# Final transposes in front of the last unit, and caches and memory laid out as the kernel uses them

## The chip, the cores and the metric

The kernel runs on one core of one Trainium2 chip. The metric is the device time of one execution in microseconds (us), lower is better. On a core several engines work side by side, each through its own queue in order: TensorE (PE; its weight loads are listed as PEld) multiplies, VectorE (DVE) and ScalarE (ACT) do elementwise work, GpSimd (POOL) does a little of it, SyncE (SP) only issues transfers. A transfer (DMA) is issued by SP, ACT or POOL and then runs on the core's 16 DMA engines. An engine that reaches an instruction whose inputs are not there waits, and everything behind it in its queue waits too.

## What is computed

Two layers of a diffusion trunk, for 128 context tokens and 128 latent tokens with the same weights. Cut to what matters here:

```
for l in range(2):
    x = x + 0.5*gate1 * swiglu(mod1(rms_norm(x)))          # FFN 1
    u = mod2(rms_norm(x)); z = u @ w_in                    # q, k, v, Fourier and mLSTM parts, gates
    context: keys and values are k, v;                      new_cache_k/v[l] = k, v
    latent:  keys = [cache_k | rope(k)], values = [cache_v | v], mLSTM starts from state_C, state_n, state_m
    p  = softmax(q1 k1) - lambda * softmax(q2 k2);  a_out = rms_norm(p @ v)
    x = x + gate2 * (sum of three gated branches) @ w_out
    x = x + 0.5*gate3 * swiglu(mod3(rms_norm(x)))          # FFN 2
y = rms_norm(x, g_final)                                   # (tokens, 1024), for both groups
```

All matrices are float32. The kernel multiplies each with the weight and the activation split into a high part (`hi`, reduced precision) and the rest (`lo`), in three products (`mm3`).

## The kernel before

**Layout and units.** Activations are kept transposed, channels on the 128 partitions, both groups' 256 tokens side by side. Weights come in chunks of mostly 1 MB (`raw`, 6 buffers) that SP loads. A chunk is cut into units; a unit is split (`split_one`) by an ACT copy (`whi`, L1523) and a DVE subtraction (`wlo`, L1524) into one of 6 pairs of buffers, and PE then runs its products: 24 of 256 columns (L166 to L168, called from `prod8`), or 12 of 512 (L760 to L762, in `aform`). A pair of buffers comes free when PE has used it, and so the ACT and DVE queues hold splits that wait for PE.

**Order.** A list of steps is recorded once, in order; each step issues its products, then refills splits. Between them, in the mixer, generators called lanes (`attn_lane`, `gate_lane`, `mlstm_lane`, `four_lane`) do the rest of the layer: at a fixed place (`mid`, half way through each unit, and after each unit) one lane is moved on to its next `yield`. What a lane issues there stands at that place in every queue. An earlier `yield` or one less therefore moves all that follows in this lane, on every engine. On DVE, steps of the adaptive modulation (L319) stand between the others.

**The mixer's start.** `first` does the four q units. `loads2` then issues on ACT's queue the loads of `cache_k` and `cache_v` (tile `ckv`) and of `state_C` (`C0`). The units k0 to k3 follow, then v0, the gates (24 products, `zgh`), v1 to v3, the Fourier units. `attn_lane` does, in this order: four PE transposes of `ckv` (half way through k2), a DVE copy of them into `kl`; `swap`, four copies from `q` into `kl` by ACT's queue, which exchange halves for the rotary step; `rope` of q on DVE, which needs them; `swap` of k, which needs the DVE to be done with `kl`; four PE transposes of k and a copy, which POOL's queue writes to `new_cache_k`; the context scores; `softmax`, whose result is `pc` (L873); four transposes of `pc`. `gate_lane` ends with eight transposes of `C0` into `c0t`. POOL's queue also loads the gate weights (`zgw`, L698).

**Transfers wait for transfers.** The transfers of SP and ACT take turns at eight semaphores. An issue waits for the transfer that used its semaphore before, in the issuing engine's queue.

**The end.** The last steps are the six units of `w_ffn2_out` for channel blocks 6 and 7. After a block's last unit, `residual` adds it to x (DVE, L570), `square` (ACT) squares it, POOL adds the square to `nsum`; block 7's stays apart (`nsq`). `block` scales y by `g_final` (DVE, L422). `fin` sums the squares on PE (L163), takes the root (`root`: DVE, then POOL), transposes the eight blocks of y for each group, 16 transposes, and scales each four of them by `rstd` on ACT or DVE into a tile that SP writes out.

Of the kernel before, what the change touches and what calls it, by code (L numbers as in the profile page):

```python
# [17 lines left out]
P = 128  # L18
D = 1024
KD = D // P  # L20
T = 128
# [101 lines left out]
def trunk_kernel(ctx: ExitStack, tc: tile.TileContext, a: dict):  # L123
# [568 lines left out]
    def add_mixer(l, norm, norm_next, mods_):  # L692
# [3 lines left out]
        def loads():  # L696
            M["zgw"] = tmp([P, KD, 16], "zgw", bufs=1)
            po.dma_start(out=M["zgw"], in_=w_in[:, 4096:4112].rearrange("(k p) f -> p k f", p=P))  # L698

        def loads2():  # L700
            ac.preload_act_table_set("natural_log_exp_and_others")
            M["ck"] = blk([P, 2, H, P], "ckv")
            nc.scalar.dma_start(out=M["ck"][:, 0], in_=a["cache_k"][0, l].rearrange("h s d -> s h d"))
            nc.scalar.dma_start(out=M["ck"][:, 1], in_=a["cache_v"][0, l].rearrange("h s d -> s h d"))
            M["C0"] = blk([P, 2, H, P], "C0")
            nc.scalar.dma_start(out=M["C0"], in_=a["state_C"][0, l].rearrange("d h v k -> v d h k"))
            gh, gl = M["gh"], M["gl"] = blk([P, KD, 104], "zgh", F32R), blk([P, KD, 104], "zgl", F32R)
            po.memset(gh.bitcast(F32), 0.0)
            po.memset(gl.bitcast(F32), 0.0)
            for gi, c0 in enumerate((0, 64, 32, 96)):  # L710
                s = M["zgw"][:, :, 4 * gi:4 * gi + 4].unsqueeze(2).to_broadcast([P, KD, 2, 4])
                hi, lo = (x[:, :, c0:c0 + 8].rearrange("p k (i h) -> p k i h", i=2) for x in (gh, gl))
                ve.tensor_copy(hi, s)
                ve.tensor_sub(lo, s, hi.bitcast(F32))
# [88 lines left out]
        def attn_lane():  # L803
            q = M["q"]
            ql = q[:, :, T:]
            kl = blk([P, H, 256], "kl")
            yield
            yield
            t = pa([P, H, P])
            for h in range(H):  # L810
                trans(t[:, h, :], M["ck"][:, 0, h, :])
            yield
            ve.tensor_copy(kl[:, :, 0:128], t)
            cosb = cst[:, C_COS:C_COS + 128].unsqueeze(1).to_broadcast([P, H, T])
# [21 lines left out]
            yield  # L836
            t = pa([P, H, P])
            for h in range(H):
                trans(t[:, h, :], k[:, h, 0:T])
            yield  # L840
            kn = t2([P, H, P], "kctx")
            ac.copy(kn, t)
            po.dma_start(out=a["new_cache_k"][0, l].rearrange("h s d -> s h d"), in_=kn)
            yield
# [115 lines left out]
            for h in range(H):  # L960
                for c in range(2):
                    vv = M["ck"][:, 1, h, :] if c == 0 else M["v"][:, 1, h * P:(h + 1) * P]
                    mm(o[:, h, :], pTl[h // 2][:, 2 * (h % 2) + c, :], vv, start=(c == 0), stop=(c == 1))
# [42 lines left out]
        def gate_lane():  # L1006
# [69 lines left out]
            for g in range(2):  # L1076
                M["w"][g] = blk([P, 2, H, T], f"w{g}")
                for d in range(2):
# [5 lines left out]
                    for h in range(H):  # L1084
                        ac.activation(M["w"][g][:, d, h, :], E[:, h, :], AF.Exp,
                                      bias=gT[:, g, 32 * d + h:32 * d + h + 1])
            yield
            c0t = M["c0t"] = blk([P, H, 2, 129], "c0t")
            ve.tensor_copy(c0t[:, :, :, 128],
                           parT[1][:, 96 + 8 * l:104 + 8 * l].rearrange("p (d h) -> p h d", d=2))  # L1090
            for d in range(2):
                t = pb([P, H, P])
                for h in range(H):
                    trans(t[:, h, :], M["C0"][:, d, h, :])
                yield
                ve.tensor_copy(c0t[:, :, d, 0:128], t)

# [345 lines left out]
    for l in range(DEPTH):  # L1443
# [3 lines left out]
        add_ffn(l, 2, norms[l, 2], norms[l + 1, 0], ADA.get((l, "ffn2")))  # L1447

    def fin():
        nf = norms[DEPTH, 0]  # L1450
        nf.stats()
        while held:
            held.pop(0)()
        outs = ("y_prompt", "y_sample")
        for i in range(2):
            for g in range(2):
                t = (pa, pm)[g]([P, 4, P])
                for r in range(4):
                    trans(t[:, r, :], nf.y[i][:, r, G[g]])
                o = t2([P, 4, P], "yo")  # L1460
                if g == 0:
                    ac.activation(o, t, AF.Copy, scale=nf.rstd[:, g:g + 1])
                else:
                    ve.tensor_scalar(o, t, nf.rstd[:, g:g + 1], None, op0=ALU.mult)  # L1464
                nc.sync.dma_start(out=a[outs[g]][0, :, i * 512:(i + 1) * 512], in_=flat(o))

    add(fin)

# [67 lines left out]
    for s in steps:  # L1536
# [16 lines left out]
        for fn in late:  # L1553
# [4 lines left out]

_INS = ["x_prompt", "x_sample", "cache_k", "cache_v", "state_C", "attn_lambda", "w_ada", "w_ffn1_in",
        "w_ffn1_out", "w_ffn2_in", "w_ffn2_out", "w_in", "w_branch_gate", "w_br_attn", "w_br_four",  # L1560
        "w_br_mlstm", "w_out"]
_OUTS = [("y_prompt", (1, T, D)), ("y_sample", (1, T, D)),
         ("new_cache_k", (1, DEPTH, H, T, 128)), ("new_cache_v", (1, DEPTH, H, T, 128)),
         ("new_state_C", (1, DEPTH, 2, H, 128, 128)), ("new_state_n", (1, DEPTH, 2, H, 128)),
# [3 lines left out]
def _arrays(inputs):  # L1568
# [6 lines left out]
    wt = inputs["w_ada"].reshape(DEPTH, D, N_MOD, KD // 2, 2, P)  # L1575
    arrays["w_adaT"] = np.ascontiguousarray(wt.transpose(0, 2, 3, 5, 4, 1))
    return arrays

# [16 lines left out]
```

## Time and profile before

| | |
|---|---|
| median of 3 runs | 1338.78 us (1338.4 to 1339.75) |
| profiled execution | 1340.14 us |
| its span (first to last instruction) | 1338.4 us |
| PE busy | 1306.4 us, 98% |
| DVE busy | 1038.2 us, 78% |
| ACT busy | 659.8 us, 49% |
| POOL busy | 68.0 us, 5% |
| moved by DMA | 304.70 MB, 228 GB/s mean |

Busy is the sum of an engine's instructions over the span. PE's products overlap, so the time one of them takes of the stream is the distance between two starts, not its own duration. A wait is listed with the instruction that ended it. PEclk is the granted clock of TensorE as a share of 2.4 GHz: 0.5 is 1.2 GHz.

### The profile page before, as it was taken

Reading aid. Unit: us, or ns where it says so; the run is one execution under the profiler, and the core shown is the slowest. Engines: PE = TensorE matmul, PEld = TensorE weight load, DVE = VectorE, ACT = ScalarE, POOL = GpSimd, SP = SyncE. Lnnn points to the kernel's source line nnn. Section 1 sums busy time; section 2 is a strip of 40 time slices with the busy share of each in tenths; the row PEclk is TensorE's granted clock in tenths of the full one; section 3 lists DMA queues with packets and bytes.
Section 4 is the critical chain, followed back from the end, with each engine's and each line's share of the span. In section 5 each row is a group of like instructions: output and inputs, shape, how many; then the busy total and the mean of one; then the engine's idle time right before and its main releaser. Section 6 shows DMA issues by size and latency. Waiting matters only on the chain. (4 is left out here: it accounts for less than half of the span.)

```text
span 1338.4 us, 25512 instructions
## 1 busy us (share of the span) xinstructions
PE 1306.4 (98%) x10584; PEld 1256.4 (94%) x10584; DVE 1038.2 (78%) x1652; ACT 659.8 (49%) x1026; POOL 68.0 (5%) x88
## 2 busy tenths in 40 slices
PE   8999999899999998999999999989999999999998
PEld 6999999788999997999999999988999899999998
DVE  5798897687678888888979988876677889895553
ACT  4654444565554454444445544455555446554442
POOL 0000001000000020000000000110000001000001
PEclk9999999899999999999999999999999999999999
DMA  9999774745567538887748977856446766495520
GB/s 377 373 336 357 242 260 163 239 139 189 190 227 260 191 130 302 277 297 264 249 155 280 302 256 252 279 167 191 158 135 200 273 228 208 164 310 188 168 96 32
DMA packets 221587, 304.70 MB, mean 228 GB/s; under 512 B 5584, under 2 KB 194272, under 8 KB 214176
## 3 DMA queue, kind: packets, MB, share of 16 engines
q1 hardware_dynamic: 213760, 295.93, 65.8%
q10 hardware_dynamic: 6640, 4.20, 1.2%
q0 software_dynamic: 1072, 2.95, 0.6%
q8 instruction: 83, 1.36, 0.4%
q14 instruction: 32, 0.26, 0.1%
HBM read 298.85 MB, written 3.15 MB: 226 GB/s over the span
## 5 line engine op out<-in xcount | busy, mean ns | idle before, releaser
L1524 DVE TENSOR_TENSOR wlo<-raw,whi 128x1024 fp32r<-128x1024 f32 (+1 forms) x428 | 507.3, 1192 | 219.3 <-ACT whi L1523 217.1
L1523 ACT CAST whi<-raw 128x1024 fp32r<-128x1024 f32 (+1 forms) x428 | 434.6, 1024 | 298.7 <-PE pm L167 211.9
L166 PE MATMUL pm<-uh,whi 128*128 128x256 f32 x1904 | 546.9, 287 | 0.0
L167 PE MATMUL pm<-ul,whi 128*128 128x256 f32 x1904 | 538.3, 283 | 1.0 <-DVE ul L495 0.9
L168 PE MATMUL pm<-uh,wlo 128*128 128x256 f32 x1904 | 538.2, 283 | 0.4 <-DVE wlo L1524 0.3
L166 PEld LDWEIGHTS pm<-uh,whi 128*128 128x128 f32 x1904 | 363.0, 191 | 12.6 <-issue 7.1
L167 PEld LDWEIGHTS pm<-ul,whi 128*128 128x128 f32 x1904 | 362.7, 190 | 2.5 <-DVE ul L495 2.1
L168 PEld LDWEIGHTS pm<-uh,wlo 128*128 128x128 f32 x1904 | 362.4, 190 | 0.9 <-DVE wlo L1524 0.8
L319 DVE CUSTOM_DVE_ANT_0 junkw<-raw,cb 128x1024 bf16<-128x1024 f32 x192 | 233.7, 1217 | 0.0
L168 PE MATMUL pm<-hh,wlo 128*128 128x256 f32 x640 | 179.6, 281 | 0.0
L166 PE MATMUL pm<-hh,whi 128*128 128x256 f32 x640 | 179.5, 280 | 0.0
L167 PE MATMUL pm<-hl,whi 128*128 128x256 f32 x640 | 179.5, 280 | 0.0
L168 PEld LDWEIGHTS pm<-hh,wlo 128*128 128x128 f32 x640 | 120.7, 189 | 0.0
L166 PEld LDWEIGHTS pm<-hh,whi 128*128 128x128 f32 x640 | 120.6, 188 | 0.0
L167 PEld LDWEIGHTS pm<-hl,whi 128*128 128x128 f32 x640 | 120.5, 188 | 0.0
L413 POOL TENSOR_TENSOR nsum<-nsum,nsq 128x256 f32<-128x256 f32 x36 | 36.1, 1002 | 816.7 <-issue 436.7
L657 ACT ACTIVATE silu<-pm 128x512 f32<-128x512 f32 x38 | 22.7, 596 | 54.9 <-PE pm L168 54.9
L411 ACT ACTIVATE nsq<-xT 128x256 f32<-128x256 f32 x42 | 17.5, 417 | 53.2 <-DVE xT L570 53.1
L177 ACT CAST hh<-silu 128x512 fp32r<-128x512 f32 x37 | 22.8, 620 | 41.4 <-DVE silu L659 41.4
L570 DVE SCALAR_TENSOR_TENSOR xT<-pm,mod,xT 128x128 f32<-128x128 f32 x96 | 28.7, 342 | 17.4 <-PE pm L168 17.3
L760 PE MATMUL pm<-whi,uh 128*128 128x512 f32 x96 | 39.3, 410 | 0.0
L761 PE MATMUL pm<-wlo,uh 128*128 128x512 f32 x96 | 37.9, 395 | 0.0
(339 smaller groups left out, 1751.4 us busy)
## 6 DMA issues: line engine op xcount, KB each, us to landing
raw<-w_ffn_in SPq DMA_DIRECT2D x82, 1024.0 KB, 6.8
raw<-w_adaT SPq DMA_DIRECT2D x48, 1024.0 KB, 5.0
raw<-w_ffn_out SPq DMA_DIRECT2D x32, 1024.0 KB, 5.0
raw<-w_in SPq DMA_DIRECT2D x32, 1024.0 KB, 5.8
raw<-w_ada SPq DMA_DIRECT2D x24, 1024.0 KB, 6.9
raw<-w_branch_gate SPq DMA_DIRECT2D x24, 1024.0 KB, 5.2
raw<-w_ffn_out SPq DMA_DIRECT2D x16, 768.0 KB, 6.0
raw<-w_out SPq DMA_DIRECT2D x8, 1024.0 KB, 5.0
```

Source lines behind the costliest of these rows:

```text
L166: pe.matmul(out, sh, mh, start=start, stop=False)
L167: pe.matmul(out, sh, ml, start=False, stop=False)
L168: pe.matmul(out, sl, mh, start=False, stop=stop)
L177: ac.copy(hi, src)
L319: ve.tensor_tensor_reduce(junkw, u.raw()[:, 0, :], cb[:, g, :], 1.0, 0.0, op0=ALU.mult, op1=ALU.add, accum_out=o[:, k, g:g + 1])
L413: eng.tensor_add(self.sum, self.sum, sq)
L570: ve.scalar_tensor_tensor(xT[:, k, G[g]], ps[:, G[g]], gate[:, k, g:g + 1], xT[:, k, G[g]], op0=ALU.mult, op1=ALU.add)
L657: ac.activation(st["s"], st["a"], AF.Silu)
L760: pe.matmul(ps[g], xh[:, G[g]], wh, start=(k == 0), stop=False)
L761: pe.matmul(ps[g], xh[:, G[g]], wl, start=False, stop=False)
L1523: ac.copy(u.hi, r)
L1524: ve.tensor_sub(u.lo, r, u.hi.bitcast(F32))
```

## The change

`cache_k`, `cache_v`, `state_C` and the gate columns of `w_in` are handed to the kernel by the host in the order in which the kernel uses them (`cache_kT`, `cache_vT`, `state_CT`, `w_inz`), and `new_cache_k` is written with channels first and turned on the host. So the transposes of `ckv`, of k and of `C0`, with their copies, are gone: `cache_kT` is loaded straight into `kl`, `state_CT` into `c0t`, and k is written out from its own tile. The gate weights and `new_cache_k` go by ACT's queue and no longer by POOL's. In `fin`, the transposes of y's first four blocks stand as a step of their own (`early`) in front of the last unit; those of blocks 4 and 5 stand between the two sums, those of blocks 6 and 7 behind them.

```
         def loads():
-            po.dma_start(out=M["zgw"], in_=w_in[:, 4096:4112].rearrange("(k p) f -> p k f", p=P))
+            nc.scalar.dma_start(out=M["zgw"], in_=a["w_inz"][l])
         def loads2():
-            M["ck"] = blk([P, 2, H, P], "ckv")
-            nc.scalar.dma_start(out=M["ck"][:, 0], in_=a["cache_k"][0, l].rearrange("h s d -> s h d"))
-            nc.scalar.dma_start(out=M["ck"][:, 1], in_=a["cache_v"][0, l].rearrange("h s d -> s h d"))
-            M["C0"] = blk([P, 2, H, P], "C0")
-            nc.scalar.dma_start(out=M["C0"], in_=a["state_C"][0, l].rearrange("d h v k -> v d h k"))
+            M["cv"] = blk([P, H, P], "cv")
+            nc.scalar.dma_start(out=M["cv"], in_=a["cache_vT"][l])
+            M["c0t"] = blk([P, H, 2, 129], "c0t")
+            nc.scalar.dma_start(out=M["c0t"][:, :, :, 0:128], in_=a["state_CT"][l])
...
             kl = blk([P, H, 256], "kl")
-            yield
-            yield
-            t = pa([P, H, P])
-            for h in range(H):
-                trans(t[:, h, :], M["ck"][:, 0, h, :])
-            yield
-            ve.tensor_copy(kl[:, :, 0:128], t)
+            nc.scalar.dma_start(out=kl[:, :, 0:128], in_=a["cache_kT"][l])
+            yield
+            yield
...
             swap(k[:, :, T:])
             yield
-            t = pa([P, H, P])
-            for h in range(H):
-                trans(t[:, h, :], k[:, h, 0:T])
-            yield
-            kn = t2([P, H, P], "kctx")
-            ac.copy(kn, t)
-            po.dma_start(out=a["new_cache_k"][0, l].rearrange("h s d -> s h d"), in_=kn)
+            nc.scalar.dma_start(out=a["new_cache_k"][0, l], in_=k[:, :, 0:T])
             yield
...
-            c0t = M["c0t"] = blk([P, H, 2, 129], "c0t")
+            c0t = M["c0t"]
...
-            for d in range(2):
-                t = pb([P, H, P])
-                for h in range(H):
-                    trans(t[:, h, :], M["C0"][:, d, h, :])
-                yield
-                ve.tensor_copy(c0t[:, :, d, 0:128], t)
...
+    def turn(i, g, rs):
+        if (i, g) not in yT:
+            yT[i, g] = (pa if i == 0 else (pd, pb)[g])([P, 4, P])
+        for r in rs:
+            trans(yT[i, g][:, r, :], norms[DEPTH, 0].y[i][:, r, G[g]])
+    def early():
+        for g in range(2):
+            turn(0, g, range(4))
     def fin():
         nf = norms[DEPTH, 0]
-        nf.stats()
+        ss = pb([P, 2])
+        for g in range(2):
+            mm(ss[:, g:g + 1], nf.sum[:, G[g]], ones[:, 0:1], start=g == 0, stop=False)
+        for g in range(2):
+            turn(1, g, (0, 1))
         while held:
             held.pop(0)()
+        for g in range(2):
+            mm(ss[:, g:g + 1], nf.last[:, G[g]], ones[:, 0:1], start=False, stop=g == 1)
+        for g in range(2):
+            turn(1, g, (2, 3))
+        nf.root(ss)
...
-                t = (pa, pm)[g]([P, 4, P])
-                for r in range(4):
-                    trans(t[:, r, :], nf.y[i][:, r, G[g]])
+                t = yT[i, g]
...
+    steps.insert(len(steps) - 1, Step(early, pump=False))
     add(fin)
```

On DVE in the first layer's mixer, where the context softmax ends (`pc`) beside the gate lane (`gpk`, whose running sums and maxima are the rows from a 40x256 operation to the 8x128 ones), before:

```order
L1037 SCALAR_TENSOR_TENSOR gpk_3080<-gpk_3080,gb 40x256
L1041 SCALAR_TENSOR_TENSOR gpk_3080<-gpk_3080 8x128
L1041 SCALAR_TENSOR_TENSOR gpk_3080<-gpk_3080,gb 8x128
L1041 SCALAR_TENSOR_TENSOR gpk_3080<-gpk_3080 8x128
L1041 SCALAR_TENSOR_TENSOR gpk_3080<-gpk_3080,gb 8x128
L1524 TENSOR_TENSOR wlo<-raw_2956,whi 128x1024
L319 ISA junkw,mod_7_103<-raw_2841,cb 128x1024
L319 ISA mod_7_103 128x1
L868 RECIPROCAL rs<-sm 128x8
L870 TENSOR_TENSOR cf<-sm,rs 128x4
L871 TENSOR_SCALAR cf<-cf,lamn 128x4
L873 SCALAR_TENSOR_TENSOR pc<-e_3177,cf,pc 128x128 x4
```

and after:

```order
L1528 TENSOR_TENSOR wlo<-raw_2876,whi 128x1024
L857 RECIPROCAL rs<-sm 128x8
L859 TENSOR_TENSOR cf<-sm,rs 128x4
L860 TENSOR_SCALAR cf<-cf,lamn 128x4
L862 SCALAR_TENSOR_TENSOR pc<-e_3143,cf,pc 128x128 x4
L1026 SCALAR_TENSOR_TENSOR gpk_3074<-gpk_3074,gb 40x256
L1030 SCALAR_TENSOR_TENSOR gpk_3074<-gpk_3074 8x128
L1030 SCALAR_TENSOR_TENSOR gpk_3074<-gpk_3074,gb 8x128
L1030 SCALAR_TENSOR_TENSOR gpk_3074<-gpk_3074 8x128
L1030 SCALAR_TENSOR_TENSOR gpk_3074<-gpk_3074,gb 8x128
L1528 TENSOR_TENSOR wlo<-raw_2956,whi 128x1024
```

The attention lane is ahead by one place: the gate lane's five operations, a split and a modulation step that stood in front of `pc` stand behind it.

On PE at the end of the program, behind the last unit (`pm<-hhl` are its last products; `y` are the scaled blocks), before:

```order
L168 MATMUL pm<-hhl_14531,wlo 128x256
L163 MATMUL pb<-ones,nsum 128x1
L163 MATMUL pb<-ones,nsq 128x1
L163 MATMUL pb<-ones,nsum 128x1
L163 MATMUL pb<-ones,nsq 128x1
L171 MATMUL pa<-cst,y_14684 128x128 x4
L171 MATMUL pm<-cst,y_14684 128x128 x4
L171 MATMUL pa<-cst,y_14685 128x128 x4
L171 MATMUL pm<-cst,y_14685 128x128 x4
```

and after:

```order
L168 MATMUL pm<-hhl_14479,wlo 128x256
L163 MATMUL pb<-ones,nsum 128x1 x2
L171 MATMUL pd<-cst,y_14633 128x128 x2
L171 MATMUL pb<-cst,y_14633 128x128 x2
L163 MATMUL pb<-ones,nsq 128x1 x2
L171 MATMUL pd<-cst,y_14633 128x128 x2
L171 MATMUL pb<-cst,y_14633 128x128 x2
```

Of the 16 transposes eight are left here, four of them in front of the sums of the last square; the other eight stand ahead of the 18 products of the last unit.

## Rows read from the trace of the kernel before

**Rows 1.** The page, engines: busy time, share of the span, instructions.

```profile
PE 1306.4 (98%) x10584; PEld 1256.4 (94%) x10584; DVE 1038.2 (78%) x1652; ACT 659.8 (49%) x1026; POOL 68.0 (5%) x88
```

**Rows 2.** Waits of PE, whole span: us in total, times, longest.

```profile
PE pa L171 <- DMA ckv<-cache_k: 9.6, 2, 4.9
PE pa L171 <- DVE pc L873: 3.3, 2, 1.6
...
PE pb L171 <- DVE ha L1192: 1.6, 2, 0.9
```

**Rows 3.** Timeline of PE, first layer's mixer: start, duration, instruction [idle before].

```profile
238.45 0.28 PE L168 MATMUL pm<-uh,wlo 128*128 128x256 f32 x1
...
244.39 0.56 PE L166 MATMUL pm<-uh,whi 128*128 128x256 f32 x1
...
248.92 0.28 PE L166 MATMUL pm<-uh,whi 128*128 128x256 f32 x1
...
250.71 0.40 PE L760 MATMUL pm<-whi,uh 128*128 128x512 f32 x1
```

**Rows 4.** The same place in the second layer.

```profile
894.07 0.28 PE L168 MATMUL pm<-uh,wlo 128*128 128x256 f32 x1
...
899.75 0.56 PE L166 MATMUL pm<-uh,whi 128*128 128x256 f32 x1
...
904.28 0.28 PE L166 MATMUL pm<-uh,whi 128*128 128x256 f32 x1
```

**Rows 5.** Timeline of PE: the transposes of k in the stream.

```profile
257.48 0.39 PE L762 MATMUL pm<-whi,ul 128*128 128x512 f32 x1
257.71 0.60 PE L171 MATMUL pa<-cst,k 128*128 128x128 f32 x4
...
258.38 0.39 PE L761 MATMUL pm<-wlo,uh 128*128 128x512 f32 x1
```

**Rows 6.** Timeline of PE: the transposes of `pc`, first layer.

```profile
279.74 0.28 PE L168 MATMUL pm<-uh,wlo 128*128 128x256 f32 x1
281.66 1.12 PE L171 MATMUL pa<-cst,pc 128*128 128x128 f32 x4 [1.65 <-DVE pc L873]
282.54 0.36 PE L166 MATMUL pm<-uh,whi 128*128 128x256 f32 x1
...
286.39 0.28 PE L167 MATMUL pm<-ul,whi 128*128 128x256 f32 x1
```

**Rows 7.** Timeline of ACT's queue (ACTq issues transfers), ACT and DVE, first layer.

```profile
247.24 3.62 ACTq L822 DMA_DIRECT2D kl<-q  x4
...
256.19 2.62 ACTq L822 DMA_DIRECT2D kl<-k  x4
258.86 1.05 ACT L1523 CAST whi<-raw 128x1024 fp32r<-128x1024 f32 x1 [6.41 <-PE pa L171]
...
244.01 2.35 DVE L1524 TENSOR_TENSOR wlo<-raw,whi 128x1024 fp32r<-128x1024 f32 x2
...
254.70 0.69 DVE L827 TENSOR_TENSOR kl<-kl,cst 128x512 f32<-128x512 f32 x1 [0.40 <-DMA kl<-q]
```

**Rows 8.** Busy time by stretch: PE, PEld, DVE, ACT, POOL, PEclk, DMA share, GB/s.

```profile
258.86:281.66 22.80, 21.16 (x112) 17.22 (x110) 18.09 (x33) 15.49 (x34) 1.56 (x2) 1.00 0.54 169
240.00:245.00 5.00, 1.35 (x7) 1.38 (x8) 4.58 (x11) 4.88 (x6) 0.00 (x0) 0.70 1.09 323
315.00:320.00 5.00, 5.00 (x25) 3.98 (x25) 3.99 (x6) 4.42 (x13) 0.00 (x0) 1.00 0.33 108
```

**Rows 9.** The chain that ended last, and POOL's timeline, at the end.

```profile
1328.77 0.62 DVE xT L570 x2
...
1329.94 0.83 PE pb L163 x6
...
1334.24 0.75 DVE yo L1464
...
1331.05 0.75 POOL L465 TENSOR_TENSOR rstd<-var,expo 128x2 f32<-128x2 f32 x1 [2.45 <-DVE var L463]
```

More of the change, by code (lines that the diff above doesn't have):

```diff
@@ L961, in attn_lane @@
                 for c in range(2):
-                    vv = M["ck"][:, 1, h, :] if c == 0 else M["v"][:, 1, h * P:(h + 1) * P]
+                    vv = M["cv"][:, h, :] if c == 0 else M["v"][:, 1, h * P:(h + 1) * P]
                     mm(o[:, h, :], pTl[h // 2][:, 2 * (h % 2) + c, :], vv, start=(c == 0), stop=(c == 1))
@@ L1447, in trunk_kernel @@
         add_ffn(l, 2, norms[l, 2], norms[l + 1, 0], ADA.get((l, "ffn2")))
+    yT = {}
+    def turn(i, g, rs):
[6 more added lines that the diff above has]
+            turn(0, g, range(4))
     def fin():
         nf = norms[DEPTH, 0]
-        nf.stats()
+        ss = pb([P, 2])
[3 more added lines that the diff above has]
+            turn(1, g, (0, 1))
         while held:
             held.pop(0)()
+        for g in range(2):
[3 more added lines that the diff above has]
+        nf.root(ss)
         outs = ("y_prompt", "y_sample")
@@ L1556, in trunk_kernel @@
     assert not any(lanes)
-_INS = ["x_prompt", "x_sample", "cache_k", "cache_v", "state_C", "attn_lambda", "w_ada", "w_ffn1_in",
+_INS = ["x_prompt", "x_sample", "attn_lambda", "w_ada", "w_ffn1_in",
         "w_ffn1_out", "w_ffn2_in", "w_ffn2_out", "w_in", "w_branch_gate", "w_br_attn", "w_br_four",
@@ L1562 @@
 _OUTS = [("y_prompt", (1, T, D)), ("y_sample", (1, T, D)),
-         ("new_cache_k", (1, DEPTH, H, T, 128)), ("new_cache_v", (1, DEPTH, H, T, 128)),
+         ("new_cache_k", (1, DEPTH, 128, H, T)), ("new_cache_v", (1, DEPTH, H, T, 128)),
          ("new_state_C", (1, DEPTH, 2, H, 128, 128)), ("new_state_n", (1, DEPTH, 2, H, 128)),
@@ L1576, in _arrays @@
     arrays["w_adaT"] = np.ascontiguousarray(wt.transpose(0, 2, 3, 5, 4, 1))
+    wz = inputs["w_in"][:, :, 4096:4112].reshape(DEPTH, KD, P, 16)
+    arrays["w_inz"] = np.ascontiguousarray(wz.transpose(0, 2, 1, 3))
+    arrays["cache_kT"] = np.ascontiguousarray(inputs["cache_k"][0].transpose(0, 3, 1, 2))
+    arrays["cache_vT"] = np.ascontiguousarray(inputs["cache_v"][0].transpose(0, 2, 1, 3))
+    arrays["state_CT"] = np.ascontiguousarray(inputs["state_C"][0].transpose(0, 4, 2, 1, 3))
     return arrays
@@ L1593 @@
     r = run_bass_kernel_spmd(nc, [arrays], core_ids=[0])
-    return tuple(r.results[0][n] for n, _ in _OUTS)
+    out = {n: r.results[0][n] for n, _ in _OUTS}
+    out["new_cache_k"] = out["new_cache_k"].transpose(0, 1, 3, 4, 2)
+    return tuple(out[n] for n, _ in _OUTS)
```

## Prediction

> **What bounds the kernel now.** I read the engines' totals first, then the waits of TensorE, then the timeline where they lie. TensorE is busy 98% of the span [rows 1], so a change is worth what it takes out of TensorE's stream and out of its waits; work saved on VectorE, ScalarE or GpSimd counts only where TensorE waits for them. Of these waits one pair stands out: the transposes of the context keys wait for the load of `cache_k`, 4.9 us at most and 9.6 us in the two layers, and in each layer those of `pc` wait 1.6 us for VectorE [rows 2]. The timeline shows a second price of such a wait. Behind the first one the 21 products from 244.39 to 248.92 take 4.53 us, 0.216 us each, the next 15 up to 250.71 take 1.79 us, 0.119 us each [rows 3]. That is TensorE at 1.2 and at 2.4 GHz: in the 5 us around the wait, in which TensorE is busy for 1.35 us, the granted clock is 0.70 on average [rows 8].
>
> **The stall for `cache_k` goes.** Nothing on TensorE reads the loaded keys in `kl` before the latent scores, far behind. From the last product ahead of the wait to the first product of 512 columns 12.26 us pass (238.45 to 250.71) [rows 3]. What stays in between is that product and 36 more (half of k2, all of k3), 37 x 0.119 = 4.40 us: gain 7.86 us, the four transposes included. In the second layer, over a shorter stretch, 894.07 to 904.28 is 10.21 us for 22 products, 2.62 us: gain 7.59 us [rows 4]. Together 15.45 us.
>
> **The other transposes of the mixer.** Products of 512 columns start 0.23 us apart (257.48 to 257.71); from 257.71 to 258.38 one of them and four transposes take 0.67 us, so four cost 0.44 us [rows 5]. Eight of k and sixteen of `C0` go, six times four: 2.64 us. Their copies on ScalarE and VectorE lie beside TensorE's work and count nothing by themselves. `state_CT` is loaded at the mixer's start and used late in the mixer; that load is hidden as `C0`'s was.
>
> **The wait for `pc` stays, and its size is the open term.** Today TensorE wants `pc` at 279.86 (279.74 plus 0.12), gets it at 281.66, needs 0.88 us for four transposes instead of 0.44, and then 3.85 us for 19 products (282.54 to 286.39) that are worth 2.26 us [rows 6]: 1.80 + 0.44 + 1.59 = 3.8 us a layer. After the change TensorE comes earlier. From 242.85 on there stand 90 products of 512 columns (v0, v1, v2 and v3, Fourier units 0 to 2, half of the next), 24 of the gates and eight score products, which I price as two fours: 90 x 0.233 + 24 x 0.119 + 0.9 = 24.7, so it wants `pc` at 267.6. The other side is a chain over three queues. The four rotary copies of q are issued at 247.24 to 250.86, VectorE goes on with them at 254.70, and only then can ScalarE's queue issue those of k, 2.62 us from 256.19; until 258.86 no split runs [rows 7]. In the new order the fourth copy of q waits for the load of `cache_v`, since it takes its semaphore. That load now stands where that of `cache_k` stood, and I let it land when that did, near 243.6; an issue is 0.65 us (2.62/4) and the landing came 3.8 us after the last issue [rows 7], so 248.1. VectorE has its two subtractions up to 246.36 and two more of the same (2.35 us), then the first rotary operation (0.69): 249.4. Two more of these and the copies of k (2.62) free ScalarE at 253.4. From there to `pc` today pass 22.8 us with VectorE busy for 18.09 in 33 instructions [rows 8]. Out of this stretch the new order takes a subtraction and a modulation step of the same size (1.18 each) and five small operations of the gate lane (no row of their own; a little under the stretch's mean of 0.55 each, 2.3): 13.4 us stay. ScalarE's first split adds 1.05; if VectorE never pauses, `pc` comes at 253.4 + 14.4 = 267.8, and the wait is nearly nothing. If the copies land 2 us later and all of today's pauses stay (22.8 - 4.7 = 18.1), it comes at 273.5, a wait of 5.9 us. No row is nearer to one end, since half of the pauses are splits that wait for TensorE, which then is ahead. I take the middle, 2.8 us, 1.0 us more than now in each layer, with the same slow stretch behind it: **-2.0 us**, between +7.7 (gone, with its slow products) and -8.
>
> A rule of the Trainium skill bears on this term. The Trainium skill, DMA: Bandwidth & Descriptors, section "Issuing engines are not separate DMA queues", says that transfers started from different engines run on the same 16 DMA engines and interleave. The row of 240 to 245 agrees: DMA share 1.09 at 323 GB/s with two engines issuing [rows 8]. By it the copies of q, now issued behind 1 MB of caches and beside two weight loads, land late; that is the second rival.
>
> **The wait for `ha`.** The transposes of the mLSTM output wait 1.6 us in two places [rows 2]. In the new order eight products of 512 columns (the modulation's, L163) stand between the last products that feed the second of them and the transposes, beside the 72 products of today; I price them like others of that width, 1.9 us, more than the longest wait of 0.9. Gain 1.6, between 0 and 1.6.
>
> **The end.** Eight transposes ahead of the last unit cost 2 x 0.44 = 0.88. Behind it today: residual at 1328.77, six sum products from 1329.94 (0.83), root on GpSimd at 1331.05 (0.75), last scaling 1334.24 to 1334.99 [rows 9]. After the change two sum products instead of six stand behind the square, 0.55 us less. The root ends at 1331.80 + 0.88 - 0.55 = 1332.13. Four transposes lie in TensorE's wait for the square (0.9 us before 1329.94), the last four beside the root. Two scalings in a row (1.5) then end at 1333.63, 1.36 us earlier. SyncE issues the four writes one behind the other, which I let take back 0.3: **+1.1 us**, between 0 and 1.4. The two scalings of y on VectorE now stand ahead of the variance; the square and its sum cover them.
>
> A rule of the Trainium skill speaks against this edit. The profile shows four transposes amid products without a fall: granted clock 1.00 in 315 to 320, where the first four of `C0` lie [rows 8]. The Trainium skill, TensorE: Matmul & The Clock Gate, section "Part 4: PE-mode transpose", says that a transpose does not count as busy TensorE as a product does. By it eight in a row could put the last unit at 1.2 GHz. Its 18 products then cost 18 x 0.097 = 1.7 us more, and the sum ends at 1321.7; the row with four speaks against it.
>
> **Transfers that move.** `zgw` and `new_cache_k` leave GpSimd's queue, where nobody waits, and add an issue of 0.65 us each to ScalarE's, which is busy for half of the span and loses the copy of k. The second waits in that queue for the weight load that used its semaphore before, and ScalarE's next splits are behind it; I put this at 0 here, and a longer hold is the third rival.
>
> **The sum**, against the profiled execution (1340.14 us, of which the span is 1338.4): 15.45 + 2.64 - 2.0 + 1.6 + 1.1 = 18.8 us, that is 1321.3. The median of the runs is 1.36 us below the profiled one, so I predict **1320.0**.
>
> **Rivals.** (1) *The wait for `pc` goes too*: VectorE does not pause. For it speaks the shorter chain, against it that VectorE was the last there in both layers. 18.8 + 2.0 + 7.7 = 28.5: 1310.3. (2) *The copies land late*: `pc` comes at 273.5 or the splits behind it hold TensorE earlier, which is the same loss. 3.1 us more in each layer: 1326.2. (3) *ScalarE is held at the new write of k*, and it becomes slower than before: TensorE has splits for six units and wants the seventh at 242.85 + 72 x 0.233 + 2.86 + 0.9 = 263.4, so up to some 8 us beyond 253.4 cost nothing. To eat 18.8 us the hold must pass 17 us in each layer; at 20 us, 12 us come back in each, 1344. In the mixers no product waits for a weight load today. (4) *The clock falls at the eight transposes*: 1321.7, above. (5) *The loads are not early enough*, so that TensorE waits for `kl` later instead: the latent scores come tens of us behind the issue, which excludes it as a case of its own.
>
> **How the numbers follow.** Forecast 0.60 (1316 to 1324 by the bounds of `ha`, the end and half of those of `pc`), rival 1 0.13, rival 2 0.17, rival 4 0.05, rival 3 0.03, no change 0.02. The range leaves out a tenth on each side: the far half of rival 1 below and that of rival 2, with rival 3, above: 1313 to 1327. A measurement of this kernel can tell about 0.2%, 2.7 us, from no change. Faster 0.95, within it 0.02, slower 0.03.
>
> **What would show it.** Right: no wait for a load in the mixer's first units; the product of 512 columns that began 12.3 us after the last one ahead of the wait begins after 4.4; ScalarE's first split behind the copies of k some 10.5 us behind that place; a wait of 1 to 4 us for `pc` with 1.2 GHz behind it; no wait for `ha`; last scaling 1.1 us closer to the last unit's end. Wrong: a wait for `pc` of 0 or above 5 us, a new wait of TensorE for a split or a PSUM copy in the Fourier units, or the last 18 products at 0.216 us each.

## The result, and the profile of the changed kernel

The changed kernel takes 1331.18 us in the median (1329.18 to 1333.25) against 1338.8 us of the kernel before: ratio 0.9942, 95% interval 0.9921 to 0.9963. It is faster by 7.6 us, 0.6%, where 18.8 us were forecast, and it lies above the range. The profiled execution took 1329.18 us with a span of 1327.4, 11.0 us less than that of before.

The waits of TensorE in the whole span (us in total, times, longest), to be read beside [rows 2]:

```profile
PE pa L171 <- DVE pc L862: 6.3, 2, 3.7
PE pb L171 <- DVE ha L1175: 3.5, 2, 2.0
PE pd L163 <- DMA raw<-w_ada: 3.0, 3, 1.6
...
PE pm L759 <- ACT v L769: 1.2, 2, 0.6
```

The wait for `cache_k`, 9.6 us, is gone. The waits for `pc` and `ha`, 3.3 and 1.6 us before, have both about doubled, and one is new: a product that needs a PSUM tile which ScalarE has not yet copied out (`v`, L769).

The timeline of TensorE in the first layer (start, duration, instruction, idle before), the place of [rows 3] and [rows 6]:

```profile
238.18 0.28 PE L168 MATMUL pm<-uh,wlo 128*128 128x256 f32 x1
...
242.55 0.39 PE L759 MATMUL pm<-whi,uh 128*128 128x512 f32 x1
...
259.00 0.40 PE L761 MATMUL pm<-whi,ul 128*128 128x512 f32 x1
259.93 0.50 PE L759 MATMUL pm<-whi,uh 128*128 128x512 f32 x1 [0.53 <-ACT v L769]
...
268.17 0.39 PE L761 MATMUL pm<-whi,ul 128*128 128x512 f32 x1
271.08 1.17 PE L171 MATMUL pa<-cst,pc 128*128 128x128 f32 x4 [2.52 <-DVE pc L862]
271.90 0.77 PE L759 MATMUL pm<-whi,uh 128*128 128x512 f32 x1
272.47 0.63 PE L760 MATMUL pm<-wlo,uh 128*128 128x512 f32 x1
```

From the last product ahead of the old wait to the first of 512 columns 4.37 us pass; they were 12.26, and 4.40 were forecast. At 259.00 the next product comes 0.93 us later instead of 0.23. At 268.40 (268.17 and 0.23) TensorE wants `pc`, which comes 2.7 us later; behind it products of 512 columns start 0.43 us apart instead of 0.23, that is, at 1.2 GHz.

The two kernels run the same weight products in the same order, and so the start of each can be compared. How far the changed kernel is ahead at some of them (start before, start after):

| place | before | after | ahead | step |
|---|---|---|---|---|
| begin of the first FFN | 16.51 | 16.24 | 0.27 | +0.3 |
| layer 1, past the stall and the transposes of k | 258.85 | 250.28 | 8.57 | +8.3 |
| layer 1, past the wait for `v`'s copy | 267.80 | 259.93 | 7.87 | -0.7 |
| layer 1, past `pc` and the slow stretch | 307.92 | 301.04 | 6.88 | -1.0 |
| layer 1, past the transposes of `C0` | 388.95 | 381.21 | 7.74 | +0.9 |
| layer 1, past `ha` | 427.25 | 421.19 | 6.06 | -1.7 |
| FFN 2, past the wait for `w_ada` | 534.93 | 527.13 | 7.80 | +1.7 |
| layer 2, ahead of the stall | 893.83 | 886.92 | 6.91 | -0.9 |
| layer 2, past the stall and k | 914.19 | 899.25 | 14.94 | +8.0 |
| layer 2, past `v`'s copy | 923.16 | 908.95 | 14.21 | -0.7 |
| layer 2, past `pc` | 963.23 | 952.14 | 11.09 | -3.1 |
| layer 2, past `C0` | 1044.17 | 1032.29 | 11.88 | +0.8 |
| layer 2, past `ha` | 1082.91 | 1071.49 | 11.42 | -0.5 |
| ahead of the early transposes of y | 1326.10 | 1315.12 | 10.98 | -0.4 |
| last unit, third product from the end | 1328.22 | 1318.11 | 10.11 | -0.9 |
| end of the span | 1338.4 | 1327.4 | 11.0 | +0.9 |

### The profile page after: what moved, and what is told of

It is laid out like the page before. It is cut to its first block, busy times and chain, and to the rows that moved or that the text cites. A ratio compares the mean times of both kernels' runs of the same rounds, so it can differ in the third digit from the quotient of the medians.

```text
span 1327.4 us, 25450 instructions
## 1 busy us (share of the span) xinstructions
PE 1299.2 (98%) x10551; PEld 1248.9 (94%) x10552; DVE 1033.7 (78%) x1646; ACT 657.4 (50%) x1024; POOL 63.9 (5%) x84
## 5 line engine op out<-in xcount | busy, mean ns | idle before, releaser
L319 DVE CUSTOM_DVE_ANT_0 junkw<-raw,cb 128x1024 bf16<-128x1024 f32 x192 | 233.5, 1216 | 0.0
```

The lines of the kernel that those rows point to most:

```text
L319: ve.tensor_tensor_reduce(junkw, u.raw()[:, 0, :], cb[:, g, :], 1.0, 0.0, op0=ALU.mult, op1=ALU.add, accum_out=o[:, k, g:g + 1])
```

## Experiments

### What the executions differ by

Label `again` is the changed kernel once more.

> The changed kernel itself, to see whether its times fall into two groups (1329.2 and 1329.4 against 1333.0 and 1333.3) also here, and where a slower execution loses its 3.8 us. If the two groups come from the clock, a slower one has a further stretch of products 0.21 us apart, 4 us of it for 2 us, behind one of the waits for ha (2.0 and 1.5 us) that today has none. If they come from a transfer, one of the waits for a weight of the modulation (1.1 and 1.6 us at 518) is longer instead.

Median 1331.43 us over 6 runs (1328.71 to 1332.32), ratio 0.9949 (0.9930 to 0.9968). Its profiled execution (1332.02 us) waits for `pc` and `ha` as the first did, with nothing slower behind `ha`. It loses 3.0 us more than the first at one place, the border of the layers, where TensorE waits for two weights of the modulation:

```profile
519.74 1.06 PE L163 MATMUL pd<-raw,cT 128*32 128x512 f32 x8 [2.01 <-DMA raw<-w_ada]
...
523.64 1.93 PE L163 MATMUL pd<-raw,cT 128*32 128x512 f32 x8 [2.83 <-DMA raw<-w_ada]
```

These were 1.10 and 1.63 us in the first profile; the rest of the 3.0 us is products at the lower clock behind them. So in this execution it is a transfer, not the clock behind `ha`; the kernel before has the same wait (its runs of this study spread from 1333.4 to 1342.3). In the profiled execution of before it was long, in that of after short: 1.7 of the 11.0 us are this, by luck, and no merit of the change.

### The edit of the end alone

`tail_only`: the kernel before, with the new functions `turn`, `early` and `fin`, and the step that calls `early`:

```
+    steps.insert(len(steps) - 1, Step(early, pump=False))
     add(fin)
```

> The kernel before with the edit of the end alone. The prediction gave it 1.1 us. From the trace of the changed kernel I now expect nothing, 1338.8 within 0.5: the last scaling ends 1.9 us closer to the last product, but the eight transposes ahead of the last unit take 0.8 us, four writes one behind the other on SyncE take 0.7 us back, and they land 0.4 us later. The rival, a clock that falls at the eight transposes, gives 1.7 us more, 1340.5.

1339.27 us over 12 runs, ratio 1.0012 (0.9997 to 1.0027): no gain. The forecast's 1.1 us (0.9992) lie outside the interval. The profile of the changed kernel shows where they stay (the timeline from the eight early transposes on):

```profile
1315.47 1.04 PE L171 MATMUL pa<-cst,y 128*128 128x128 f32 x8
1316.26 0.36 PE L166 MATMUL pm<-hh,whi 128*128 128x256 f32 x1
...
1318.34 0.28 PE L168 MATMUL pm<-hhl,wlo 128*128 128x256 f32 x1
...
1321.44 0.69 ACT L1465 ACTIVATE yo<-pa,rstd 128x512 f32<-128x512 f32 x1 [1.67 <-POOL rstd L465]
...
1322.11 0.74 DVE L1467 TENSOR_SCALAR yo<-pb,rstd 128x512 f32<-128x512 f32 x1
...
1322.16 0.36 SPq L1468 DMA_DIRECT2D y_prompt<-yo  x1
...
1323.59 0.39 SPq L1468 DMA_DIRECT2D y_sample<-yo  x1
```

The last scaling ends at 1322.85, but the fourth issue begins at 1323.59, since the four follow each other on SyncE by 0.48 us, and the span ends 3.8 us behind it. What sets the end behind an issue, `half_written` asked, the changed kernel without the first two of its four writes of y:

```
+                if i == 1:
                     nc.sync.dma_start(out=a[outs[g]][0, :, i * 512:(i + 1) * 512], in_=flat(o))
```

> The changed kernel without the first two of its four writes of y (channels 0 to 511 are left out), all else as it is. It asks what sets the end behind the last scaling. If it is the writes themselves (1 MB from the first issue on: 5.2 us in the changed kernel, 5.3 with the issues on two queues, 5.9 before), the span ends 3.5 us or less after the last issue, and 1 us or more closer to the last transposes than the 6.9 us of the changed kernel: 5.9 or less. If it is a fixed time behind the last issue (3.8 us there), it ends 3.8 us behind it, 6.0 to 6.4 us behind the last transposes.

```profile
1325.24 0.36 SPq L1469 DMA_DIRECT2D y_prompt<-yo  x1
1325.66 0.42 SPq L1469 DMA_DIRECT2D y_sample<-yo  x1
```

The span ends at 1329.2, 3.6 us behind the last issue and 6.2 behind the last transposes (1323.05; 6.8 in the changed kernel, from 1320.54). That is between the two expectations and nearer to the second. In the kernel before, whose four issues spread over 2.5 us, the end comes 3.4 us behind the last (1335.02 to 1338.4); in the changed kernel they spread over 1.4 us, and it comes 3.8 behind. So issues closer together are in part paid back; why, no run shows.

### The transposes of `pc` later on TensorE

`pc_later`:

```
+            yield
             t = tr4([pc[:, h, :] for h in range(H)])
             yield
             pT = ev4(t)
             while "v" not in M:
                 yield
-            yield
```

> The changed kernel with the transposes of pc one unit (12 products of 512 columns, 2.8 us, and eight of zfour) later on TensorE, and nothing else moved but the copy behind them. Theory: TensorE waits for pc (2.5 and 3.7 us) because the attention lane is one place ahead on TensorE while VectorE's chain is as long as it was. Then both waits vanish or are under 0.3 us, the 1.2 GHz stretches behind them too, and the time falls by some 4.5 us in the first layer and 6.5 in the second: 1318 to 1321 against 1329 to 1333. Rival: the wait hides that splits are late, and TensorE waits for a split instead within the next 5 us: 1326 or more.

1336.04 us over 12 runs (ratio to before 0.9982): 4.6 us slower than the changed kernel. The wait for `pc` is gone, and a longer one stands right behind it. The waits of TensorE, and ScalarE's timeline:

```profile
PE pa L163 <- ACT pT L875: 9.1, 2, 4.8
```

```profile
277.54 0.42 ACT L1042 ACTIVATE g<-gpk 36x256 f32<-36x256 f32 x1 [5.05 <-DVE gpk L1033]
...
280.71 0.58 ACT L875 COPY pT<-pa 128x512 f32<-128x512 f32 x1
```

The copy `pT` now stands behind the gate lane's exponentials, for which ScalarE waits 5 us until VectorE has made `gpk`. The chain on VectorE and ScalarE as a whole is late, and a later place for one step of it hands the wait to the next. The theory that the place of these transposes is to blame fell.

### The cached keys alone, with every place kept

`keys_alone`: the kernel before, with

```
             kl = blk([P, H, 256], "kl")
+            nc.scalar.dma_start(out=kl[:, :, 0:128], in_=a["cache_kT"][l])
             yield
             yield
-            t = pa([P, H, P])
-            for h in range(H):
-                trans(t[:, h, :], M["ck"][:, 0, h, :])
             yield
-            ve.tensor_copy(kl[:, :, 0:128], t)
```

> The kernel before with one part of the change alone: the cached keys are loaded straight into kl, and their transposes and copy are gone, but the empty place stays, so that everything else of the attention lane stands where it stood on every engine; the transposes of k and of the state stay too. It separates the removal of the stall from the move of the lane. The stall is worth 15.4 us with its transposes. If the move is what makes pc later than TensorE wants it, then here TensorE wants it one unit (2.8 us) later, the wait is about the 1.7 us of before, and nearly all of the 15.4 us stay: 1323 to 1325 against 1338. If the wait is made by VectorE's chain in whatever place (TensorE comes 7.9 us earlier and the chain does not), pc is waited for by several us here too, as in the changed kernel or longer: 1327 to 1332.

1330.65 us, ratio 0.9930 (0.9913 to 0.9947): of the 15.4 us 8.5 are left. The wait for `pc` stays about as it was (2.8 us in all), as the first theory said, but the loss is there all the same, in a wait that neither named:

```profile
PE pa L163 <- ACT kctx L838: 4.6, 2, 2.9
```

`kctx`, ScalarE's copy of the transposed k, stands behind the rotary copies of k in ScalarE's queue. So with every place kept most of the loss is there too: where the stall goes, TensorE meets a ScalarE that is held at these copies (here it makes no split for 7.5 us).

### The rotary copies of k from GpSimd's queue

The hold can be seen in the changed kernel (ACTq issues transfers; then ACT and DVE):

```profile
243.37 0.59 ACTq L817 DMA_DIRECT2D kl<-q  x1
...
251.66 2.62 ACTq L817 DMA_DIRECT2D kl<-k  x4
254.32 1.05 ACT L1527 CAST whi<-raw 128x1024 fp32r<-128x1024 f32 x1 [7.28 <-issue]
...
250.17 0.69 DVE L822 TENSOR_TENSOR kl<-kl,cst 128x512 f32<-128x512 f32 x1 [1.19 <-DMA kl<-q]
...
255.40 1.23 DVE L1528 TENSOR_TENSOR wlo<-raw,whi 128x1024 fp32r<-128x1024 f32 x1 [3.82 <-ACT whi L1527]
...
270.58 1.14 DVE L862 SCALAR_TENSOR_TENSOR pc<-e,cf,pc 128x128 f32<-128x128 f32 x4
```

For 7.3 us ScalarE does nothing but wait to issue four copies whose result is read tens of us later, and VectorE, which then makes `pc`, idles 3.8 us behind it. `k_swap_gpsimd` takes them off this queue:

```
-            def swap(src):
+            def swap(src, eng=nc.scalar):
...
-                    nc.scalar.dma_start(out=sw[o], in_=src[i])
+                    eng.dma_start(out=sw[o], in_=src[i])
...
-            swap(k[:, :, T:])
+            swap(k[:, :, T:], po)
```

> The changed kernel with the four rotary copies of k issued from GpSimd's queue instead of ScalarE's. Nothing waits for them for tens of us; in the changed kernel they hold ScalarE's queue until VectorE has rotated q, so that ScalarE splits nothing for 7.3 us and VectorE idles 3.8 us behind. Theory: this hold, on top of the attention lane's earlier place, makes pc late. Without it pc comes some 3.5 us earlier in each layer, the waits of 2.5 and 3.7 us and the 1.2 GHz behind them go, and so does the wait of 0.6 us for the copy of v; 1320 to 1323 against 1331. Rival from the run that moved the transposes of pc: the next thing on ScalarE or VectorE is late too (pT behind the gate lane's exponentials, which wait for VectorE's scans), and TensorE waits there instead: 1327 or more. Second rival: issues from GpSimd slow VectorE, no gain.

1324.18 us (1323.15 to 1324.49), ratio 0.9895 (0.9882 to 0.9908): 7.0 to 7.3 us faster than the two medians of the changed kernel, which were measured on other chips (6.3 to 7.2 by the ratios to the kernel before), and 1.2 us above the expectation. ScalarE goes on with splits, `pc` comes 2.7 us earlier, the wait for `v`'s copy is gone, and that for `pc` falls from 6.3 to 2.5 us:

```profile
246.22 2.00 ACT L1527 CAST whi<-raw 128x1024 fp32r<-128x1024 f32 x2
...
267.85 1.14 DVE L862 SCALAR_TENSOR_TENSOR pc<-e,cf,pc 128x128 f32<-128x128 f32 x4
```

```profile
PE pa L171 <- DVE pc L862: 2.5, 2, 2.1
```

What is left is nearly all in the second layer. The edit also takes four issues out of the turns at the eight semaphores; no run separates this from the hold. In this run the clock fell behind the first layer's wait for `ha`, which at 2.05 us is as long as in the changed kernel (2.04), where it did not fall; the last section has the rows. That costs some 1.1 us here.

### The loads behind the copies of q

`loads_behind` moves the loads of `cache_vT`, `state_CT` and `cache_kT` behind `swap(ql)` in ScalarE's queue; `both` adds the copies of k on GpSimd's queue; `loads_gpsimd` puts the loads on GpSimd's queue too, with `ha` later (below). The core of the first:

```
-            nc.scalar.dma_start(out=kl[:, :, 0:128], in_=a["cache_kT"][l])
             yield
             yield
...
             swap(ql)
+            nc.scalar.dma_start(out=kl[:, :, 0:128], in_=a["cache_kT"][l])
+            nc.scalar.dma_start(out=M["cv"], in_=a["cache_vT"][l])
+            nc.scalar.dma_start(out=M["c0t"][:, :, :, 0:128], in_=a["state_CT"][l])
```

> The changed kernel with the three loads of caches and state behind the rotary copies of q in ScalarE's queue, not in front of them. In the changed kernel the last copy lands 6.2 us after its issue (3.8 before), and VectorE idles 1.2 us for it. Theory (the prediction's second rival in a small size): transfers in front of the copies delay them; behind them, VectorE does not wait, pc comes 1.2 us earlier in each layer, and 2 to 4 us are gained: 1327 to 1329. Rival: the copies wait for the semaphores of weight loads in either order, and the landing stays: no gain, 1331.

> The two edits together: k's copies on GpSimd's queue and the loads behind q's copies. If the two holds add up, pc comes 4.7 us earlier, and 1319 to 1322 results. If VectorE's own work of about 18 us is the limit, no more than the copies of k on GpSimd's queue alone.

> The faster candidate (k's copies on GpSimd's queue, ha's second transposes a unit later; the writes of y as in the changed kernel), with the three loads of caches and state on GpSimd's queue as well, the keys' load behind q's copies. Theory: in the runs with the loads behind q's copies, ScalarE's queue was held 5.1 us by an issue (state_CT) that waits for the transfer which used its semaphore before, a weight load. On GpSimd's queue no issue holds ScalarE, and q's copies no longer stand behind loads: the wait of VectorE for them (1.0 to 1.7 us) goes, and the remaining wait of 1.6 us for pc in the second layer falls by that: 1314 to 1317 against 1317.7. Rival: the loads still share the DMA engines with the copies, or the copies of q then meet other semaphores: 1318 or more.

`loads_behind` took 1336.54 us, 5 us more than the changed kernel, and `both` 1331.04, 7 us more than the copies of k alone. In the new order the issue of `state_CT` takes the semaphore of a load of `w_in` that hasn't landed, and ScalarE stands (ScalarE's timeline in the first and in the second layer, then TensorE's waits):

```profile
248.80 0.58 ACTq L825 DMA_DIRECT2D c0t<-state_CT  x1
249.49 1.05 ACT L1527 CAST whi<-raw 128x1024 fp32r<-128x1024 f32 x1 [5.06 <-DMA cv<-cache_vT]
...
905.49 1.05 ACT L1527 CAST whi<-raw 128x1024 fp32r<-128x1024 f32 x1 [4.65 <-DMA raw<-w_in]
```

The second layer's row names the weight load. The first names `cache_vT`, which lands at the same time; the issue itself follows the landing of the load of `w_in` by 0.02 us.

```profile
PE pm L757 <- ACT v L767: 8.4, 2, 4.4
```

These waits have two holds ahead of them, that of `state_CT` and behind it that of the copies of k (6.0 us in the first layer). In `both`, without the second hold, the wait for `v`'s copy is 2.0 us, in the second layer alone, where `state_CT` holds ScalarE for 7.2 us; that for `pc` is 6.0 us in all there.

In `loads_gpsimd` no issue holds ScalarE, and VectorE no longer waits for q's copies. It took 1319.94 us (1315.78 to 1322.39), no better than the candidate below (1317.67 and 1318.49). So the delay of the copies is real (6.2 us from the last issue to VectorE's use in the changed kernel, 3.8 before), but its price is nothing that these runs can tell. The Trainium skill, DMA: Bandwidth & Descriptors, section "Issuing engines are not separate DMA queues", says that transfers of several engines run on the same 16 DMA engines and interleave; the delay agrees with that.

### The second transposes of `ha` later

```
                 ve.tensor_mul(ha, ha, ss.unsqueeze(2).to_broadcast([P, H, P]))
                 yield
                 yield
+                if g == 1:
+                    yield
+                    yield
```

> The changed kernel with the second transposes of ha in each layer one unit (24 products, 2.8 us) later. Theory: the wait of 2.0 and 1.5 us is the place, and vanishes; if the clock does not fall behind it, 3.5 us are gained: 1326 to 1329.5. If the slower group of executions comes from a clock that falls behind this wait, that group vanishes too and the runs lie within 1 us. Rival: what follows on the lane (the last branch needs ha's result) comes late by the same 2.8 us and TensorE waits there: no gain.

1327.08 us (1324.77 to 1329.42), ratio 0.9920 (0.9900 to 0.9939): 4.3 us faster than `again` on the same chip. The wait for `ha` is gone, and nothing waits in its stead. The runs still lie 4.7 us apart: this wait is not what spreads them, and `again` shows one place that does.

### The second layer's modulation step

In the changed kernel `pc` is waited for 1.2 us longer in the second layer. There a step of the modulation (L319) stands on VectorE right in front of it:

```profile
918.91 1.22 DVE L319 CUSTOM_DVE_ANT_0 junkw<-raw,cb 128x1024 bf16<-128x1024 f32 x1
...
920.06 0.20 DVE L857 RECIPROCAL rs<-sm 128x8 f32<-128x8 f32 x1
```

`mod_step` sets the rate `win`, by which such steps are strewn over the mixer's first units, from 0.30 to 0.29:

```
-RATE = {"in0": 0.93, "in": 0.85, "out": 0.75, "win": 0.3, "branch": 0.35, "last": 0.5, "merge": 0.0}
+RATE = {"in0": 0.93, "in": 0.85, "out": 0.75, "win": 0.29, "branch": 0.35, "last": 0.5, "merge": 0.0}
```

> The changed kernel with the rate at which the modulation steps are strewn over the mixer's first units lowered from 0.30 to 0.29, so that in the second layer, too, one and not two of these steps stands on VectorE between the rotation of q and pc (a step is 1.2 us); other modulation steps move a unit later with it. Theory: the second wait for pc falls from 3.7 to 2.5 us, that of the first layer. Rival: it stays at 3.7. The whole time is not expected to show it, since other steps move as well: 1329 to 1333.

The second wait fell from 3.73 to 1.04 us, further than expected, and the wait for `v`'s copy ahead of it grew from 0.62 to 1.89: TensorE has lost the rest there. The two together fell by 1.4. The time is 1327.12 us (1326.4 to 1328.9), below the 1329 to 1333 expected and some 4 us less than the changed kernel on other chips; a large part of that comes from the border of the layers (3.2 us against the first profile of the changed kernel), where TensorE now waits 1.2 us for `w_ada` in all and not 2.7 to 4.8: with the lower rate the modulation's weights are loaded in another order there.

### A faster kernel

`combined`: the copies of k from GpSimd's queue, `ha` later, and the writes of `y_prompt` from ScalarE's queue. `combined_2` is the same again, `combined_mod` has the rate 0.29 too. Beside the edits shown above:

```
-                nc.sync.dma_start(out=a[outs[g]][0, :, i * 512:(i + 1) * 512], in_=flat(o))
+                (nc.scalar, nc.sync)[g].dma_start(out=a[outs[g]][0, :, i * 512:(i + 1) * 512], in_=flat(o))
```

> A candidate for a faster kernel: k's copies on GpSimd's queue, the second transposes of ha one unit later (4.3 us alone), and the two writes of y_prompt issued from ScalarE's queue. The writes: the last issue comes 0.7 us earlier, gain 0.5 to 0.8. If all add up, 1315 to 1318.

> The faster candidate again, beside the run above on the same chip: 1316 to 1319.

> The faster candidate with the same rate. The waits of 0.3 and 1.6 us for pc become 0.3 and 0.4 or less: 1315 to 1318, 1.2 us below the candidate, if the steps that move with it cost nothing elsewhere.

1317.67 us (ratio 0.9843, 0.9826 to 0.9859) and, on another chip, 1318.49 (0.9853); with the rate 0.29 beside the latter 1312.85 us (1312.17 to 1313.85), ratio 0.9810 (0.9792 to 0.9828). Both beat both kernels. The two writes from ScalarE's queue brought nothing: the span ends 6.9 us behind the last transposes, 6.8 without them. The last issue comes 0.3 us earlier, but the end comes 4.2 us behind it and not 3.8. Of the 5.6 us by the rate 1.2 come from `pc`, where the waits are 0.35 and 0.44 us:

```profile
PE pa L171 <- DVE pc L862: 0.8, 2, 0.4
```

The larger part comes again from the border of the layers (6.6 us in the profiled pair, of which other places take some back), by an effect on the order of loads that I had not meant; the 1312.85 us lie below the expectation for this reason.

## Why the prediction was wrong, step by step

| term | forecast | profiled pair |
|---|---|---|
| stall for `cache_k` with the transposes of k | 15.45 + 0.88 | 16.3 |
| transposes of `C0` | 1.76 | 1.7 |
| wait for `pc` | -2.0 | -4.1 (-1.0, -3.1) |
| wait for `v`'s copy | not seen | -1.4 |
| wait for `ha` | +1.6 | -2.1 |
| the end | +1.1 | 0.0 |
| `w_ada`, the begin, and stretches that didn't change | 0 | +0.7 |
| sum | 18.8 | 11.1 |

The right-hand numbers are the steps of the table above, and their sum is the 11.0 us up to rounding. The median moved 3.4 us less than the profiled pair; half of that may be the wait for `w_ada`, which was 1.7 us kinder to the profiled execution of after than to that of before. What makes the rest I don't know.

The savings came as forecast; the waits did not. By size the forecast is off by 3.7 us at `ha`, 2.1 at `pc`, 1.4 at `v`'s copy and 1.1 at the end.

**Right:** the stall's price with its slow products, to 0.1 us; what transposes cost in a stream; the first layer's wait for `pc` (forecast 2.8, measured 2.7, and 1.0 us of loss in the lead). The last is luck: no row spoke for a place between the two ends, 0.2 and 5.9 us, whose middle is 3.0, and both sides came later than forecast. TensorE wanted `pc` at 268.40 and not 267.6. ScalarE was free at 254.32 and not 253.4: VectorE could use the copies of q only 6.2 us behind their last issue, where the forecast had 3.8. The clock did not fall at the eight transposes: the 18 products behind them (1316.26 to 1318.34) start 0.12 us apart, that is, at 2.4 GHz. By the rule of the Trainium skill, TensorE: Matmul & The Clock Gate, section "Part 4: PE-mode transpose", that was a rival; this row speaks against it.

**The second layer's `pc`.** The step that failed is "the new order takes a subtraction and a modulation step" out of the stretch, "in each layer". I had read it off the first layer's order and doubled it. In the second layer the modulation step stays; the wait is 3.7 us and the loss 2.1 us larger:

```profile
921.25 1.17 PE L171 MATMUL pa<-cst,pc 128*128 128x128 f32 x4 [3.73 <-DVE pc L862]
```

`mod_step`, which takes this step away from there, brings the wait to 1.0 us, though part of that went over to `v`'s copy.

**`v`'s copy.** The failing step is "up to some 8 us beyond 253.4 cost nothing". It counts only the splits that TensorE has in stock. But ScalarE also empties PSUM tiles, and the first product of the Fourier units needs the one with `v`, wanted at 259.23; with ScalarE free at 254.32 and its queue in order the copy came late. The forecast had named a new wait of TensorE for a PSUM copy in the Fourier units as a sign of being wrong, and this is one. In `loads_behind` a second hold of 5.1 us ahead of the first makes the wait 4.4 us. That ScalarE is held at an issue, as rival 3 has it, therefore costs far earlier than I had let it. At the write of `new_cache_k`, where I had put the hold, there is none (an issue of 0.65 us).

**`ha`.** The failing step is "I price them like others of that width, 1.9 us". I measured the slack on TensorE, from the last mLSTM products to the transposes. It did grow, but in between lies a chain over three engines, whose steps are issued at places of their own (DVE, ACT and DVE again; then TensorE):

```profile
403.12 0.71 PE L163 MATMUL pb<-mv,w 128*128 128x129 f32 x4
...
409.29 0.42 DVE L1142 TENSOR_TENSOR nB<-nB,pb 128x258 f32<-128x258 f32 x1
...
412.06 1.03 ACT L1527 CAST whi<-raw 128x1024 fp32r<-128x1024 f32 x1
...
413.12 1.23 DVE L1528 TENSOR_TENSOR wlo<-raw,whi 128x1024 fp32r<-128x1024 f32 x1 [1.90 <-ACT whi L1527]
414.26 0.16 DVE L1172 TENSOR_SCALAR mss<-mss 128x4 f32<-128x4 f32 x1
415.61 0.69 DVE L1175 TENSOR_TENSOR ha<-ha,mss 128x512 f32<-128x512 f32 x1 [1.19 <-POOL mss L1173]
...
414.13 0.28 PE L168 MATMUL pm<-ah,wlo 128*128 128x256 f32 x1
416.45 0.63 PE L171 MATMUL pb<-cst,ha 128*128 128x128 f32 x4 [2.04 <-DVE ha L1175]
```

Before, the chain began 0.9 us behind the start of the products that feed it:

```profile
417.04 0.61 PE L163 MATMUL pb<-mv,w 128*128 128x129 f32 x4
...
417.97 0.41 DVE L1159 TENSOR_TENSOR nB<-nB,pb 128x258 f32<-128x258 f32 x1
```

Now it begins 6.2 us behind them (409.29 behind 403.12). The eight products of the modulation stand ahead of the chain's first step, not behind it, and in the chain a split and GpSimd's power stand in the way. More slack on TensorE gave the chain nothing.

**The end.** The failing step is "SyncE issues the four writes one behind the other, which I let take back 0.3". The last scaling ends 2.0 us closer to the last unit (6.5 us behind the start of its last product before, 4.5 after); the issues take back 0.7 and the denser writes 0.4, and 0.9 are paid ahead of the last unit. Before, the last product and the last issue were:

```profile
1328.45 0.28 PE L168 MATMUL pm<-hhl,wlo 128*128 128x256 f32 x1
...
1335.02 0.33 SPq L1465 DMA_DIRECT2D y_sample<-yo  x1
```

**What was behind it.** The sum priced each wait as if the others stood still. ScalarE is held at the copies of k in the kernel before too, 6.41 us up to 258.86 [rows 7]. The change brings the end of that hold forward by 4.5 us, to 254.32; TensorE, without the stall, comes forward by 8.6 us. So TensorE reaches what ScalarE and VectorE make behind the hold, `v`'s copy and `pc`, 4 us sooner against them than before. Without the hold 7.0 to 7.3 us came back (`k_swap_gpsimd`), and 4.3 us in `ha_later`. That these two together are near the 11.2 us by which the forecast missed is chance: 7.7 of the 11.2 are its terms, 3.4 the difference between profiled pair and medians, and the two edits also remove waits that the forecast had kept. The two edits add up and a little more: `combined` is 12.7 to 13.8 us below the medians of the changed kernel. One reason is the slow stretch behind `ha` that `k_swap_gpsimd` still has and `combined` has not.

## What to carry to other kernels

A stall of the bounding engine is cover for everything that the other engines do meanwhile: before its whole length is counted as gain, look at whether what the others hand over behind it comes forward by as much, and take away the holds that keep it back. A transfer that must wait for a result belongs on a queue that has nothing else to do, not on an engine that feeds the bounding one. A wait that is moved by a place is not removed: follow the chain behind it over all engines, in every repetition of the loop by itself.

## What the runs showed of the hardware

- An issue on ScalarE's queue can hold the engine for 5.1 us (7.2 in `both`) though its data are ready, because a weight load of SyncE holds its semaphore. Which issue is struck changes with the order of issues (`loads_behind`, where `state_CT` takes the semaphore of a load of `w_in`).
- How long TensorE idled did not settle by itself what its clock did next. In the changed kernel it fell behind the 2.5 us for `pc` and not behind the 2.0 us for `ha`; in `k_swap_gpsimd` it fell behind the same wait for `ha`, 2.05 us long. The three stretches behind these waits, with the mean granted clock (0.62, 1.00 and 0.70, where 1.00 is 2.4 GHz and 0.50 is 1.2) as the number ahead of the last two:

```profile
271.08:275.60 4.52, 4.52 (x17) 3.63 (x18) 4.37 (x10) 0.76 (x2) 0.00 (x0) 0.62 0.74 231
416.45:420.00 3.55, 3.55 (x30) 3.55 (x31) 3.55 (x5) 0.00 (x0) 0.00 (x0) 1.00 0.39 96
412.19:415.74 3.55, 3.55 (x23) 3.55 (x24) 3.55 (x5) 0.00 (x0) 0.00 (x0) 0.70 0.29 81
```

  It also fell there in `loads_behind` and `both` (0.52 each), and not in `again`, `half_written`, `mod_step` and `pc_later`, with waits of 2.04 or 2.05 us in all of them. What decides is not shown.
- Behind the last of the four writes' issues 3.4 us pass until the end of the span in the kernel before, 3.8 in the changed kernel and 4.2 in `combined`, where two queues issue them. The closer the four issues lie, the longer it is: they spread over 2.5, 1.4 and 1.2 us.
